# The seam before an output projection: the first tile's order written out, w_out rows staged in output tiles

## The chip, the cores and the metric

The kernel runs on one core of a Trainium2 chip. The metric is the device time of one execution in microseconds. All times below are of this core; the profile is one execution, recorded by the hardware profiler.

## What is computed

One layer of a hybrid backbone, on two inputs: a context of 256 tokens and a latent grid of 2048 tokens, each of width 1024. Both share all weights. Per input:

```python
h = rms_norm(x, g_pre) * (1 + scale) + shift
u = h @ w_in
z, xbc, dt_raw, ga, gb, gsil = jnp.split(u, [I_Z, I_XBC, I_DT, I_GA, I_GB], axis=-1)
y_ssd, h_fin = ssd_branch(z, xbc, dt_raw, ...)        # two scans, forward and backward; rms_norm
y_conf = conformer_branch(ga, gb, ...) * silu(gsil)   # depthwise conv; layer_norm; silu
out = concatenate([y_ssd, y_conf], axis=-1) @ w_out   # 2048 rows of w_out
return x + gate * rms_norm(out, g_post), h_fin
```

The scan runs over chunks of 128 tokens, in both directions. The outputs are the two results and the final scan states of the context. All is float32; each product of the large projections is split into a high and a low half, so that it takes three matmuls (high by high, high by low, low by high).

## The kernel before, in words

The tokens make 18 tiles of 128: tiles 0 and 1 are the context, 2 to 17 the latent grid. For the input projection they are grouped into five blocks (`TOK`, `BNS`, lines 28 and 29): block 0 has 256 tokens, blocks 1 to 4 have 512 each. Block 4 holds tiles 14 to 17, block 3 tiles 10 to 13. Blocks 1, 2 and 0 form the first half, 3 and 4 the second (`ORDER`, line 30). The normalized input of a block (`hh`, `hl`) sits in one of three memory slots, `SLOT` (line 31).

The input projection runs in units, one for each 128 columns of w_in. `silu_unit` (line 560) is the kind that comes last: for each block it runs 24 matmuls of 512 columns into the PSUM tile `sp` and yields after each three, then ScalarE (tanh) and VectorE make the result `sth`, which is stored to DRAM: `ZS` for z, `GS` for the gate. The other work of the time (convolutions, the forward scan) is interleaved with the units' matmuls.

The second pass over the tiles goes backward, `order` = 17, 16, ..., 2, 1, 0 (line 1087). A tile needs, in this pass:

- `ssd_load`, `st_load`: load the scan's pieces `ct`, `el` (twice), `y`, `z` and the chunk state `st`.
- `state_mm` (16 matmuls into `qo`), `y_state`, `y_gate`, `y_sum`: the backward scan's part, gated by z, and the sum of squares `zr`. `state_decay` and `state_add` carry the backward state `Sb` on.
- `conf_load` (`cn`), `conf_sum`, `conf_mean` (matmul `cm`), `conf_centre`, `conf_square`, `conf_sqsum` (`nq`): the layer norm of the other branch.
- `norms` (matmul `pm`, then small VectorE steps and a power on GpSimd), `spread` (matmul `pn`), then `ssd_scale`, `conf_scale`, `conf_silu`, `conf_gate` with the gate `gs_load` loads from `GS`.
- `hl` and `lo`: ScalarE casts the high half, VectorE subtracts for the low half. The result is `yh`, `yl` for the first eight rows of w_out and `ph`, `pl` for the last eight.
- `out_part`: for each of the 16 row groups of w_out, `k`, six matmuls into the PSUM tiles `op`.
- `finish_squares`, `finish_power`, `finish_gate`, `finish_add`: the last norm, the residual and the store.

`load_wo` (line 965) loads row group `k` of w_out into a staging tile `wst` (512 KB) and splits it into `woh` (ScalarE) and `wol` (VectorE). The staging tiles share the tags `yh` and `yl` of pool `p0`. Groups 0 to 8 are loaded during the last units, 9 to 15 after them (lines 1224 and 1225), when the pools of the units are closed and pools `p3` and `wo4` take their memory. Some memory is shared this way at an earlier point also: pool `p2`, which holds the conf tiles, opens when slot 1 is closed, after the first of the two blocks of the last units.

Until line 1243 the compiler orders the instructions of each engine, by priority in program order and a simulated time. From there on (`V.on = S.on = T.on = True`) VectorE, ScalarE and TensorE keep the order of the program, written out in the loop over `order`: the matmuls of tile `i` are cut into pieces, and between them stand the steps of the next tile (`nxt`) and the one after it (`nx2`). The DMAs of the sync queue are not in that list and stay ordered by the compiler. The first tile of the loop, 17, is prepared before it, and so are the scan's and the conf branch's sums of tile 16. The final backward state of the context is written out after the loop by `state_out` (line 1316): eight transposes, two copies on ScalarE, two stores.

Of the kernel before, what the change touches and what calls it, by code (L numbers as in the profile page):

```python
# [17 lines left out]
P = 128  # L18
D = 1024
# [8 lines left out]
TOK = (0, 256, 768, 1280, 1792)  # L28
BNS = (256, 512, 512, 512, 512)
ORDER = ((1, 2, 0), (3, 4))  # L30
SLOT = (0, 1, 2, 1, 2)
RAWO = (2, 260, 772, 130, 642)
NF = 3
PREP = 16
# [27 lines left out]
def take(gen, n):  # L62
    for _ in range(n):
        yield next(gen, None)
# [16 lines left out]
def backbone_kernel(ctx, tc, xa, xt_in, cols, rows, wconv, conf_b, gp_row, bg_row, state0, w_mod, w_dt, w_in, w_out,  # L81
# [796 lines left out]
    def run(gen):  # L878
        for _ in gen:
            pass  # L880
# [36 lines left out]
    xbc_phase(0, first, hb, [hprep(2, hb), hprep(0, hb)], tails, dt_post(0))  # L917
    extra = chain([gate_rows()] + [ctx_conv(j, big) for j in range(4)])
    interleave(post(0, 6), merge(scan(range(9)), 68, extra, 9 + 4 * 13), 90 * 8)
    last = [silu_unit(0, GS0, GS, j, hb, (1, 2, 0)) for j in (6, 7)]  # L920
    prep = hprep(3, hb)
    s = 0
    for b in range(3):
# [38 lines left out]
    p0 = ph_1.enter_context(tc.tile_pool(name="p0", bufs=1))  # L962
    WH, WL = {}, {}

    def load_wo(k, pool):
        wl = pool.tile([P, D], F32R, name=f"wol{k}", tag=f"wol{k}")
        wh = pool.tile([P, D], F32R, name=f"woh{k}", tag=f"woh{k}")
        wr = p0.tile([P, D], F32, tag=("yh", "yl")[k % 2], name=f"wst{k}", bufs=2)
        DMA.dma_start(wr, w_out[k * P:(k + 1) * P, :])
        if k < 8:  # L970
            g = cv[:, C_NORMG + k:C_NORMG + k + 1]
            S.activation(wh, wr, AF.Copy, scale=g)
            V.scalar_tensor_tensor(wl, wr, g, wh.bitcast(F32), MUL, SUB)
        else:
            S.copy(wh, wr)
            V.tensor_tensor(wl, wr, wh.bitcast(F32), SUB)
        WH[k], WL[k] = wh, wl

    y8 = lambda t: t.rearrange("p (q l) -> p q l", l=P)
    Sb = [p0.tile([P, 512], F32, name=f"Sb{g}") for g in range(2)]  # L980
# [42 lines left out]
    def state_add(i):  # L1023
        for g in range(2):
            sg = sl[i]["st"][:, g * 512:(g + 1) * 512]
            if i == NCTX - 1:
                V.tensor_copy(Sb[g], sg)
            else:
                V.tensor_tensor(Sb[g], Sb[g], sg, ADD)
# [21 lines left out]
    def ssd_scale(i, y, pb):  # L1051
        V.tensor_tensor(y, y, rows8(pb[:, 0:P]), MUL)
# [14 lines left out]
    def spread(i, rs):  # L1067
        pb = bank("ss", f"pn{i}")
        for c, r in rs:
            T.matmul(pb[:, c * P:(c + 1) * P], r.to_broadcast([P, P]), ident, start=True, stop=True)  # L1070
        return pb
# [7 lines left out]
    def lo(t):  # L1079
        V.tensor_tensor(t[1], t[2], t[0].bitcast(F32), SUB)  # L1080

    for k in range(6):
        load_wo(k, wo1)
        run(take(blocks, 5))
    state_in(1, Sb, p0.tile([P, 8, P], F32, tag="yl", name="sti1", bufs=2))
    p1 = ph_1.enter_context(tc.tile_pool(name="p1", bufs=1))
# [9 lines left out]
    def conf_load(i):  # L1096
        n = p2.tile([P, 8, P], F32, tag="cn", name=f"cn{i}", bufs=2)
        DMA.dma_start(n, CV[:, i * P:(i + 1) * P].rearrange("(c p) t -> p c t", p=P))
        return n

    def conf_sum(i, n):
        v = p2.tile([P, 8, P], F32, tag="v", name=f"v{i}", bufs=2)
        return v, sum8(v[:, 0, :], v[:, 0:4, :], n)

    def conf_mean(i, t):
        mean = bank("ss", f"cm{i}")[:, 0:P]
        T.matmul(mean, ones, t, start=True, stop=True)
        return mean

    def conf_centre(n, mean):  # L1110
        V.scalar_tensor_tensor(n, rows8(mean), -1.0 / D, n, MUL, ADD)

    def conf_square(v, n):
        S.activation(v, n, AF.Square)
        return v

    def conf_sqsum(i, v):
        return v, sum8(p2.tile([P, P], F32, tag="nq", name=f"nq{i}", bufs=1), v[:, 0:4, :], v)

    def gs_load(i):  # L1120
        gs = p2.tile([P, 8, P], F32, tag="gs", name=f"gsl{i}", bufs=1)
        DMA.dma_start(gs, chan_slice(GS, i))
        return gs

    def conf_scale(n, pb):
        V.tensor_tensor(n, n, rows8(pb[:, P:2 * P]), MUL)
# [6 lines left out]
    def conf_gate(v, gs):  # L1133
        V.scalar_tensor_tensor(v, v, 0.5, gs, MUL, MUL)
# [55 lines left out]
    for g in range(2):  # L1190
        state_decay(i, g)
    state_add(i)
    run(take(blocks, 5))
    for k in range(6, 9):
        load_wo(k, wo2)
        run(take(blocks, 8))
    run(blocks)
    last = [silu_unit(1, GS0, GS, j, hb) for j in range(5, 8)]
    for b in range(2):
        for m, u in enumerate(last):  # L1200
            run(take(u, 8))
            if b == 0 and m == 1:
                rs = norms(i, yz, None)
            if b == 1 and m == 0:
                ssd_scale(i, yz[0], spread(i, rs))
                yh = hl(p0, "y", 2, i, yz[0])
                lo(yh)
                ph_b[1].close()
                p2 = ph_1.enter_context(tc.tile_pool(name="p2", bufs=1))
                n = conf_load(i)  # L1210
                v, t = conf_sum(i, n)
                conf_centre(n, conf_mean(i, t))
    for u in last:
        run(u)
    v, nq = conf_sqsum(i, conf_square(v, n))
    conf_scale(n, spread(i, norms(i, None, (v, nq))))
    gs = gs_load(i)
    conf_silu(n, v)
    conf_gate(v, gs)
    ph_b[2].close()  # L1220
    ph_h.close()
    p3 = ph_1.enter_context(tc.tile_pool(name="p3", bufs=1))
    wo4 = ph_1.enter_context(tc.tile_pool(name="wo4", bufs=1, side="right"))
    for k in range(9, 16):
        load_wo(k, wo4)
    load_gg(0)
    i = order[1]
    ssd_load(i)
    st_load(i)
    n = conf_load(i)  # L1230
    state_mm(i)
    y_state(i)
    y_gate(i)
    yz = y_sum(i)
    for g in range(2):
        state_decay(i, g)
    v2, t = conf_sum(i, n)
    conf_centre(n, conf_mean(i, t))
    nq = conf_sqsum(i, conf_square(v2, n))
    gs = gs_load(i)  # L1240
    ssd_load(order[2])
    n2 = conf_load(order[2])
    V.on = S.on = T.on = True
    for a, i in enumerate(order):
        last = a + 1 == NT
        nxt = order[a + 1] if a + 1 < NT else None
        nx2 = order[a + 2] if a + 2 < NT else None
        banks(i)
        pt = hl(p2, "p", 1, i, v)
        out_part(pso[i], yh, 0, 1)  # L1250
        rs = None if last else norms(nxt, yz, nq)
        if a:
            finish_squares(order[a - 1])
        lo(pt)
        out_part(pso[i], yh, 1, 4)
        if nxt is not None:
            state_add(nxt)
            pb = spread(nxt, rs)
        if nx2 is not None:
            st_load(nx2)  # L1260
            v2, t = conf_sum(nx2, n2)
        if a:
            finish_power(order[a - 1])
        out_part(pso[i], yh, 4, 5)
        if nx2 is not None:
            state_mm(nx2)
        if nxt is not None:
            y = yz[0]
            ssd_scale(nxt, y, pb)
            yhn = hl(p0, "y", 2, nxt, y)  # L1270
            conf_scale(n, pb)
            v = nq[0]
            conf_silu(n, v)
        out_part(pso[i], yh, 5, 8)
        if nx2 is not None:
            mean = conf_mean(nx2, t)
        if nxt is not None:
            lo(yhn)
        if a:
            if order[a - 1] == 1:  # L1280
                load_gg(1)
            finish_gate(order[a - 1])
        out_part(pso[i], pt, 8, 10)
        if nx2 is not None:
            y_state(nx2)
            state_decay(nx2, 0)
            conf_centre(n2, mean)
            conf_square(v2, n2)
        if nxt is not None:
            conf_gate(v, gs)  # L1290
        if nx2 is not None:
            y_gate(nx2)
            state_decay(nx2, 1)
            gs = gs_load(nx2)
            nq = conf_sqsum(nx2, v2)
        if a:
            finish_add(order[a - 1])
        if nx2 is not None:
            yz = y_sum(nx2)
        if a + 3 < NT:  # L1300
            ssd_load(order[a + 3])
            n, n2 = n2, conf_load(order[a + 3])
        else:
            n = n2
        if last:
            out_part(pso[i], pt, 10, 16, (0,))
            out_part(pso[i], pt, 10, 16, (1,))
        else:
            out_part(pso[i], pt, 10, 16)
            yh = yhn  # L1310
    finish_squares(i)
    finish_power(i)
    finish_gate(i)
    finish_add(i, True)
    V.on = S.on = T.on = False
    state_out(1, Sb, lambda n: p1.tile([P, D], F32, tag="z", name=n, bufs=2)[:, 0:512])
    ph_1.close()


# [57 lines left out]
```

## Time and profile before

| | |
|---|---|
| median of 3 runs | 1871.06 us (1869.57 to 1874.34) |
| the profiled execution's own time | 1872.28 us |
| its span, first to last instruction | 1870.5 us |
| mean granted TensorE clock | 0.984 |
| TensorE busy | 1808.1 us (97%) |
| VectorE, ScalarE, GpSimd busy | 1203.1, 863.8, 175.9 us |
| first `op` matmul, last `op` matmul | 1408.3 us, 1862.6 us |

How to read it: PE is TensorE's matmul, PEld its weight load, DVE VectorE, ACT ScalarE, POOL GpSimd, SP the engine that issues most DMAs. Busy times of an engine are sums over its instructions. A row of a timeline has the start, the length, engine and line, the operation, the tile that is written and those that are read, and, in brackets, how long the engine was idle before it and what released it. The chain of work that ended last is followed back from the end: it shows at each time the piece of work on which the end depended, and for DMA the time from issue to landing. Instructions whose order is kept from line 1243 on all carry line 77, that of the helper which records them, so they are told apart by their tiles. Matmuls overlap: one of 512 columns is recorded with 0.39 us, but they start 0.23 us apart.

### The profile page before, as it was taken

The page shows a single profiled execution, that of the slowest core. Times are in us where ns is not written, and L with a number is a line of the kernel's source. Part 1 is how long each engine was busy: PE and PEld are TensorE (multiplying, and loading weights), DVE is VectorE, ACT ScalarE, POOL GpSimd, SP SyncE. Part 2 cuts the span into 40 slices and gives each one's busy share as a digit, 9 for nine tenths or more (in the row PEclk, how much of TensorE's full clock was granted, in tenths as well). Part 3 has the DMA queues.
Part 4 walks back from the last instruction along what each step waited for, and adds up shares of the span by engine and source line. Part 5 has one row for each costly group of instructions (what it writes and reads, how often), then busy time and mean ns, then how long its engine had stood idle before and what let it go on. Part 6 is the DMA issues. An engine that isn't in the chain of part 4 may idle for free.

```text
span 1870.5 us, 30012 instructions
## 1 busy us (share of the span) xinstructions
PE 1808.1 (97%) x11223; PEld 1493.1 (80%) x11223; DVE 1203.1 (64%) x1841; ACT 863.8 (46%) x1956; POOL 175.9 (9%) x281
## 2 busy tenths in 40 slices
PE   7899999999999999999998989999997999999998
PEld 4788887788888888888876767777886888888887
DVE  2477887785555553577587845666347777777773
ACT  3646424455445441644224545553326454444441
POOL 0002001111101100100001111110000111111110
PEclk9899999999999999999999999999998999999999
DMA  8656575576566654545589798895967656666632
GB/s 298 219 199 210 203 241 181 175 254 219 195 217 211 226 196 169 167 155 189 170 200 233 199 251 229 258 244 175 331 189 209 183 167 174 172 171 178 182 106 79
DMA packets 305309, 375.22 MB, mean 201 GB/s; under 512 B 85254, under 2 KB 204678, under 8 KB 305164
## 3 DMA queue, kind: packets, MB, share of 16 engines
q1 hardware_dynamic: 284428, 335.56, 58.1%
q10 hardware_dynamic: 20736, 37.76, 7.1%
q8 instruction: 88, 1.44, 0.3%
q14 instruction: 57, 0.47, 0.1%
HBM read 243.66 MB, written 129.59 MB: 200 GB/s over the span
## 4 chain that ended last, share of the span: by engine, by line
PE 85%; DMA 7%; DVE 4%; ACT 1%; issue 1%; SPq 1%; POOL 0%; POOLq 0%; DVEq 0%; ACTq 0%
PE op L77 21%; PE sp L391 7%; PE sp L392 7%; PE sp L393 7%; PE xp L391 5%; PE xp L392 5%; PE xp L393 5%; PE ga L391 3%; PE ga L393 2%; PE ga L392 2%; PE gb L391 2%; PE gb L393 2%; PE gb L392 2%; DMA lb<-lt 2%; PE py L732 2%; DVE cg L608 2%
## 5 line engine op out<-in xcount | busy, mean ns | idle before, releaser
L696 ACT ACTIVATE lb<-lb,WB 128x128 f32<-128x128 f32 x576 | 184.3, 391 | 167.7 <-POOL lb L688 162.1
L391 PE MATMUL sp<-hh,wh 128*128 128x512 f32 (+1 forms) x640 | 238.5, 373 | 0.0
L392 PE MATMUL sp<-hl,wh 128*128 128x512 f32 (+1 forms) x640 | 236.0, 369 | 0.0
L393 PE MATMUL sp<-hh,wl 128*128 128x512 f32 (+1 forms) x640 | 235.8, 368 | 0.0
L391 PE MATMUL xp<-hh,wh 128*128 128x512 f32 (+1 forms) x480 | 179.3, 375 | 6.1 <-ACT wh L366 4.9
L688 POOL TENSOR_SCALAR_AFFINE_SELECT lb<-lb 128x512 f32<-128x512 f32 x144 | 112.6, 786 | 714.2 <-ACT el L685 366.7
L393 PE MATMUL xp<-hh,wl 128*128 128x512 f32 (+1 forms) x480 | 179.0, 373 | 0.0
L392 PE MATMUL xp<-hl,wh 128*128 128x512 f32 (+1 forms) x480 | 178.9, 373 | 0.0
L488 DVE SCALAR_TENSOR_TENSOR cva<-raw,cwh,cva 128x1280 f32<-128x1280 f32 (+1 forms) x96 | 142.1, 1488 | 19.7 <-ACT cva L482 17.9
L391 PEld LDWEIGHTS sp<-hh,wh 128*128 128x128 f32 x640 | 120.6, 189 | 20.8 <-DVE sth L568 0.4
L393 PEld LDWEIGHTS sp<-hh,wl 128*128 128x128 f32 x640 | 120.6, 188 | 20.7
L392 PEld LDWEIGHTS sp<-hl,wh 128*128 128x128 f32 x640 | 120.7, 189 | 19.8
L391 PE MATMUL ga<-hh,wh 128*128 128x512 f32 (+1 forms) x320 | 122.0, 381 | 6.8 <-DMA wh<-whd 6.3
L391 PE MATMUL gb<-hh,wh 128*128 128x512 f32 (+1 forms) x320 | 121.4, 379 | 5.3 <-DVE gth L555 5.3
L393 PE MATMUL ga<-hh,wl 128*128 128x512 f32 (+1 forms) x320 | 119.4, 373 | 0.5 <-DMA wl<-wld 0.5
L392 PE MATMUL gb<-hl,wh 128*128 128x512 f32 (+1 forms) x320 | 119.6, 374 | 0.0
L393 PE MATMUL gb<-hh,wl 128*128 128x512 f32 (+1 forms) x320 | 119.6, 374 | 0.0
L392 PE MATMUL ga<-hl,wh 128*128 128x512 f32 (+1 forms) x320 | 119.2, 373 | 0.0
L568 DVE SCALAR_TENSOR_TENSOR sth<-sth,sp 128x512 f32<-128x512 f32 (+1 forms) x80 | 50.4, 630 | 97.3 <-ACT sth L567 96.9
L391 PEld LDWEIGHTS xp<-hh,wh 128*128 128x128 f32 x480 | 92.1, 192 | 23.2 <-ACT wh L366 5.5
L608 DVE SCALAR_TENSOR_TENSOR cg<-cg,cv 128x256 f32<-128x256 f32 x240 | 107.6, 487 | 0.6
L392 PEld LDWEIGHTS xp<-hl,wh 128*128 128x128 f32 x480 | 91.7, 191 | 15.7 <-DVE hl L312 0.4
(252 smaller groups left out, 3745.8 us busy)
## 6 DMA issues: line engine op xcount, KB each, us to landing
lb<-lt ACTq DMA_DIRECT2D x144, 256.0 KB, 4.5
wr<-in_w_in SPq DMA_DIRECT2D x88, 256.0 KB, 4.7
whd<-wh SPq DMA_DIRECT2D x44, 512.0 KB, 3.6
wld<-wl SPq DMA_DIRECT2D x44, 512.0 KB, 5.2
wh<-whd SPq DMA_DIRECT2D x44, 512.0 KB, 4.6
wl<-wld SPq DMA_DIRECT2D x44, 512.0 KB, 5.8
xT<-xb SPq DMA_DIRECT2D x18, 512.0 KB, 5.0
yp<-yg SPq DMA_DIRECT2D x36, 256.0 KB, 4.3
```

Of the source, the lines that this page charges most:

```text
L77: return lambda *a, **k: self._tc.keep_in_program_order(f(*a, **k))
L391: T.matmul(ps[:, :BN], wh[:, k, :], hh[:, k, :], start=(k == 0), stop=False)
L392: T.matmul(ps[:, :BN], wh[:, k, :], hl[:, k, :], start=False, stop=False)
L393: T.matmul(ps[:, :BN], wl[:, k, :], hh[:, k, :], start=False, stop=(k == KT - 1))
L488: V.scalar_tensor_tensor(a[:, :n], raw[:, t:t + n], cwh[:, ct * 5 + t:ct * 5 + t + 1], a[:, :n], MUL, ADD)
L568: V.scalar_tensor_tensor(th, th, 1.0, ps[:, :BN], ADD, MUL)
L608: V.scalar_tensor_tensor(acc, g[:, t:t + 256], cv[:, w0 + t:w0 + t + 1], acc, MUL, ADD)
L688: G.affine_select(E[g, hq, d], E[g, hq, d], pattern=[[0, 4], [sg, P]], compare_op=ALU.is_ge, fill=NEG, base=0, channel_multiplier=-sg)
L696: S.activation(lb[:, h, :], lb[:, h, :], AF.Exp, bias=WB[:, i, c + h:c + h + 1])
L732: T.matmul(py[g][j * HD:(j + 1) * HD, q * P:(q + 1) * P], xt[g][:, h * HD:(h + 1) * HD], E[g, hq, 0][:, t, :], start=True, stop=True)
```

## The change

Four things, in one change. Blocks 3 and 4 change places: their slots are swapped, and the last units take block 4 first (in the first half, block 2 first). Tile 16's backward part and both tiles' conf sums are called in between the last units. The loop's first pass, tile 17, is written out ahead of the loop with the kept order already on, and in it stand the splits of row groups 9 to 15, which are loaded into tiles of `p3` (`gg`, `xr` and twice `o`) that the later output steps use. In the second and third tile the steps between the matmuls come later, by `e` = 4 and 2 row groups. And `state_out` is called within the last tile but one.

```diff
-SLOT = (0, 1, 2, 1, 2)
+SLOT = (0, 1, 2, 2, 1)
...
-    last = [silu_unit(0, GS0, GS, j, hb, (1, 2, 0)) for j in (6, 7)]
+    last = [silu_unit(0, GS0, GS, j, hb, (2, 1, 0)) for j in (6, 7)]
...
+    def wo_load(k, pool):
+        WL[k] = pool.tile([P, D], F32R, name=f"wol{k}", tag=f"wol{k}")
+        WH[k] = pool.tile([P, D], F32R, name=f"woh{k}", tag=f"woh{k}")
+        if k < 9:
+            wst[k] = p0.tile([P, D], F32, tag=("yh", "yl")[k % 2], name=f"wst{k}", bufs=2)
+        else:
+            tag = ("gg", "xr", "o", "o")[k % 4]
+            wst[k] = p3.tile([P, D], F32, tag=tag, name=f"wst{k}", bufs=2 if tag == "o" else 1)
+        DMA.dma_start(wst[k], w_out[k * P:(k + 1) * P, :])
...
+    i1 = order[1]
+    ssd_load(i1)
+    st_load(i1)
...
-    last = [silu_unit(1, GS0, GS, j, hb) for j in range(5, 8)]
+    last = [silu_unit(1, GS0, GS, j, hb, (4, 3)) for j in range(5, 8)]
     for b in range(2):
         for m, u in enumerate(last):
             run(take(u, 8))
             if b == 0 and m == 1:
                 rs = norms(i, yz, None)
-            if b == 1 and m == 0:
+                state_mm(i1)
+                y_state(i1)
+                y_gate(i1)
+            if b == 0 and m == 2:
                 ssd_scale(i, yz[0], spread(i, rs))
                 yh = hl(p0, "y", 2, i, yz[0])
                 lo(yh)
+                yz = y_sum(i1)
+                for g in range(2):
+                    state_decay(i1, g)
                 ph_b[1].close()
                 p2 = ph_1.enter_context(tc.tile_pool(name="p2", bufs=1))
-                n = conf_load(i)
-                v, t = conf_sum(i, n)
-                conf_centre(n, conf_mean(i, t))
+                nn = [conf_load(i), conf_load(i1)]
+                vv = [conf_sum(j, n) for j, n in zip((i, i1), nn)]
+                for (v, t), j, n in zip(vv, (i, i1), nn):
+                    conf_centre(n, conf_mean(j, t))
+                    conf_square(v, n)
+                nq = conf_sqsum(i, vv[0][0])
+            if b == 1 and m == 0:
+                rs = norms(i, None, nq)
+                nq = conf_sqsum(i1, vv[1][0])
+            if b == 1 and m == 1:
+                n, v = nn[0], vv[0][0]
+                conf_scale(n, spread(i, rs))
+                conf_silu(n, v)
+                ssd_load(order[2])
+            if b == 1 and m == 2:
+                gs0, v0, n = gs_load(i), v, nn[1]
...
-    for k in range(9, 16):
-        load_wo(k, wo4)
+    for k in range(9, 13):
+        wo_load(k, wo4)
+    n2 = conf_load(order[2])
+
+    def out_seg(i, y, p, k0, k1):
+        out_part(pso[i], y, k0, min(k1, 8))
+        out_part(pso[i], p, max(k0, 8), k1)
...
+    i, nxt, nx2 = order[:3]
+    banks(i)
+    out_part(pso[i], yh, 0, 1)
+    rs = norms(nxt, yz, nq)
+    out_part(pso[i], yh, 1, 4)
+    state_add(nxt)
+    pb = spread(nxt, rs)
+    st_load(nx2)
+    out_part(pso[i], yh, 4, 5)
+    state_mm(nx2)
+    ssd_scale(nxt, yz[0], pb)
+    yhn = hl(p0, "y", 2, nxt, yz[0])
+    conf_gate(v0, gs0)
+    pt = hl(p2, "p", 1, i, v0)
+    gs = gs_load(nxt)
+    conf_scale(n, pb)
+    lo(yhn)
+    lo(pt)
+    out_part(pso[i], yh, 5, 8)
+    for k in (9, 10):
+        wo_split(k)
+        wo_load(k + 4, wo4)
+    v = nq[0]
+    conf_silu(n, v)
+    out_part(pso[i], pt, 8, 9)
+    v2, t = conf_sum(nx2, n2)
+    wo_split(11)
+    wo_load(15, wo4)
+    for k in range(12, 15):
+        wo_split(k)
+    load_gg(0)
+    out_part(pso[i], pt, 9, 12)
+    mean = conf_mean(nx2, t)
+    y_state(nx2)
+    state_decay(nx2, 0)
+    wo_split(15)
+    conf_centre(n2, mean)
+    conf_square(v2, n2)
+    out_part(pso[i], pt, 12, 16)
+    conf_gate(v, gs)
+    y_gate(nx2)
+    state_decay(nx2, 1)
+    gs = gs_load(nx2)
+    nq = conf_sqsum(nx2, v2)
+    yz = y_sum(nx2)
...
-    for a, i in enumerate(order):
+    for a, i in enumerate(order[1:], 1):
         last = a + 1 == NT
+        e = {1: 4, 2: 2}.get(a, 0)
...
-        out_part(pso[i], yh, 0, 1)
+        out_seg(i, yh, pt, 0, 1 + e)
...
-        out_part(pso[i], pt, 8, 10)
+        out_seg(i, yh, pt, 8 + e, 10 + e)
+        if a + 2 == NT:
+            state_out(1, Sb, lambda n: p1.tile([P, D], F32, tag="z", name=n, bufs=2)[:, 0:512])
```

`wo_split(k)` is the second half of the former `load_wo`: the two instructions that make `woh` and `wol` from the staging tile. All other cuts between the pieces of the loop move by `e` in the same way, and `state_out` after the loop is gone.

More of the change, by code (lines that the diff above doesn't have):

```diff
@@ L963, in backbone_kernel, with wo_split @@
     WH, WL = {}, {}
[L965 to L969, printed above, removed]
+    wst = {}
+    def wo_load(k, pool):
[7 more added lines that the diff above has]
+        DMA.dma_start(wst[k], w_out[k * P:(k + 1) * P, :])
+    def wo_split(k):
+        wl, wh, wr = WL[k], WH[k], wst.pop(k)
         if k < 8:
@@ L976, in load_wo @@
             V.tensor_tensor(wl, wr, wh.bitcast(F32), SUB)
-        WH[k], WL[k] = wh, wl
     y8 = lambda t: t.rearrange("p (q l) -> p q l", l=P)
@@ L1082, in backbone_kernel @@
     for k in range(6):
-        load_wo(k, wo1)
+        wo_load(k, wo1)
+        wo_split(k)
         run(take(blocks, 5))
@@ L1192, in backbone_kernel @@
     state_add(i)
+    i1 = order[1]
+    ssd_load(i1)
+    st_load(i1)
     run(take(blocks, 5))
     for k in range(6, 9):
-        load_wo(k, wo2)
+        wo_load(k, wo2)
+        wo_split(k)
         run(take(blocks, 8))
     run(blocks)
-    last = [silu_unit(1, GS0, GS, j, hb) for j in range(5, 8)]
+    last = [silu_unit(1, GS0, GS, j, hb, (4, 3)) for j in range(5, 8)]
     for b in range(2):
@@ L1207, in backbone_kernel @@
                 lo(yh)
+                yz = y_sum(i1)
+                for g in range(2):
+                    state_decay(i1, g)
                 ph_b[1].close()
                 p2 = ph_1.enter_context(tc.tile_pool(name="p2", bufs=1))
-                n = conf_load(i)
-                v, t = conf_sum(i, n)
-                conf_centre(n, conf_mean(i, t))
+                nn = [conf_load(i), conf_load(i1)]
[14 more added lines that the diff above has]
+                gs0, v0, n = gs_load(i), v, nn[1]
     for u in last:
         run(u)
[L1215 to L1219, printed above, removed]
     ph_b[2].close()
@@ L1223, in backbone_kernel @@
     wo4 = ph_1.enter_context(tc.tile_pool(name="wo4", bufs=1, side="right"))
-    for k in range(9, 16):
-        load_wo(k, wo4)
-    load_gg(0)
[L1227 to L1243, printed above, removed]
-    for a, i in enumerate(order):
+    for k in range(9, 13):
[4 more added lines that the diff above has]
+        out_part(pso[i], p, max(k0, 8), k1)
+    V.on = S.on = T.on = True
+    i, nxt, nx2 = order[:3]
[18 more added lines that the diff above has]
+    for k in (9, 10):
+        wo_split(k)
+        wo_load(k + 4, wo4)
[6 more added lines that the diff above has]
+    for k in range(12, 15):
+        wo_split(k)
+    load_gg(0)
+    out_part(pso[i], pt, 9, 12)
[12 more added lines that the diff above has]
+    yz = y_sum(nx2)
+    ssd_load(order[3])
+    n, n2 = n2, conf_load(order[3])
+    yh = yhn
+    for a, i in enumerate(order[1:], 1):
         last = a + 1 == NT
+        e = {1: 4, 2: 2}.get(a, 0)
         nxt = order[a + 1] if a + 1 < NT else None
@@ L1249, in backbone_kernel @@
         pt = hl(p2, "p", 1, i, v)
-        out_part(pso[i], yh, 0, 1)
+        out_seg(i, yh, pt, 0, 1 + e)
         rs = None if last else norms(nxt, yz, nq)
-        if a:
-            finish_squares(order[a - 1])
+        finish_squares(order[a - 1])
         lo(pt)
-        out_part(pso[i], yh, 1, 4)
+        out_seg(i, yh, pt, 1 + e, 4 + e)
         if nxt is not None:
@@ L1261, in backbone_kernel @@
             v2, t = conf_sum(nx2, n2)
-        if a:
-            finish_power(order[a - 1])
-        out_part(pso[i], yh, 4, 5)
+        finish_power(order[a - 1])
+        out_seg(i, yh, pt, 4 + e, 5 + e)
         if nx2 is not None:
@@ L1273, in backbone_kernel @@
             conf_silu(n, v)
-        out_part(pso[i], yh, 5, 8)
+        out_seg(i, yh, pt, 5 + e, 8 + e)
         if nx2 is not None:
@@ L1278, in backbone_kernel @@
             lo(yhn)
[L1279 to L1282, printed above, removed]
-        out_part(pso[i], pt, 8, 10)
+        if order[a - 1] == 1:
+            load_gg(1)
+        finish_gate(order[a - 1])
+        out_seg(i, yh, pt, 8 + e, 10 + e)
+        if a + 2 == NT:
+            state_out(1, Sb, lambda n: p1.tile([P, D], F32, tag="z", name=n, bufs=2)[:, 0:512])
         if nx2 is not None:
@@ L1295, in backbone_kernel @@
             nq = conf_sqsum(nx2, v2)
-        if a:
-            finish_add(order[a - 1])
+        finish_add(order[a - 1])
         if nx2 is not None:
@@ L1308, in backbone_kernel @@
         else:
-            out_part(pso[i], pt, 10, 16)
+            out_seg(i, yh, pt, 10 + e, 16)
             yh = yhn
@@ L1315, in backbone_kernel @@
     V.on = S.on = T.on = False
-    state_out(1, Sb, lambda n: p1.tile([P, D], F32, tag="z", name=n, bufs=2)[:, 0:512])
     ph_1.close()
```

## Prediction

> **What bounds the kernel now.** I read the page's busy shares first, then TensorE busy by stretches of 10 us, then the chain of work that ended last, and last the timeline of the one place where TensorE stands still.
>
> ```profile
> PE 1808.1 (97%) x11223; PEld 1493.1 (80%) x11223; DVE 1203.1 (64%) x1841; ACT 863.8 (46%) x1956; POOL 175.9 (9%) x281
> ```
>
> TensorE is the bound: 97% of a span of 1870.5 us. Other engines matter only where they make it wait. By stretches (columns: length, busy PE, PEld, DVE, ACT, POOL, granted clock, DMA share, GB/s), every stretch from 1200 us to 1860 us holds 9.8 (the first row) to 10.0 us of TensorE work, but for the three that follow it here:
>
> ```profile
> 1340.00:1350.00 10.00, 9.80 (x48) 7.97 (x48) 4.45 (x4) 4.41 (x5) 0.00 (x0) 1.00 1.05 392
> ...
> 1400.00:1410.00 10.00, 9.06 (x51) 7.51 (x49) 6.82 (x11) 5.32 (x14) 0.55 (x1) 1.00 0.72 217
> 1410.00:1420.00 10.00, 0.00 (x0) 0.00 (x0) 6.27 (x7) 9.94 (x20) 0.00 (x0) 0.62 0.92 214
> 1420.00:1430.00 10.00, 7.80 (x30) 6.60 (x31) 7.25 (x14) 2.41 (x3) 2.12 (x2) 0.70 0.88 266
> ```
>
> This is the seam between the last projection units (tile `sp`) and the out-projection (tile `op`). The chain says why it is there, and what a settled tile costs afterwards:
>
> ```profile
> 1404.83 0.24 PE sp L393
> ...
> 1406.44 5.36 DMA gs<-sth
> ...
> 1411.85 4.33 DMA gsl<-gs
> ...
> 1417.42 2.36 DVE wol L976 x2
> ...
> 1422.20 0.98 PE pm L77 x4
> 1423.19 5.64 PE op L77 x18
> ...
> 1449.08 0.34 PE pm L77 x4
> 1449.42 4.25 PE op L77 x18
> 1453.67 0.44 PE pn L77 x4
> 1454.11 1.39 PE op L77 x6
> 1455.50 1.78 PE qo L77 x16
> 1457.29 4.12 PE op L77 x18
> 1461.41 0.22 PE cm L77 x2
> 1461.63 12.29 PE op L77 x54
> ```
>
> The last unit's result goes out to DRAM (5.36) and comes back as the gate of tile 17 (4.33); then VectorE multiplies, splits two w_out rows and sums tile 16's squares; only then can `pm` run, which stands seventh in TensorE's fixed order.
>
> ```profile
> 1406.06 0.49 PE L1070 MATMUL pn<-ident,yr 128*128 128x128 f32 x2 [0.88 <-POOL yr L148]
> ...
> 1406.38 1.95 PE L1014 MATMUL qo<-ct,Sb 128*128 128x128 f32 x16
> ...
> 1408.31 0.70 PE L77 MATMUL op<-woh,yh 128*128 128x512 f32 x2
> ...
> 1409.33 1.28 ACT L1130 ACT_TABLE_LOAD   x1
> ...
> 1410.62 3.18 ACT L1130 ACTIVATE v<-cn,cv 128x128 f32<-128x128 f32 x8
> ...
> 1422.20 0.56 PE L77 MATMUL pm<-ones,zr 128*128 128x1 f32 x2 [12.26 <-DVE zr L986]
> ```
>
> So the seam costs 0.88 + 12.26 us of waits. The restart is slow too: the granted clock is 0.62 and 0.70 there, and from `pm` to `pm` the first tile takes 1449.08 - 1422.20 = 26.88 us, where the eight settled rows sum to 24.83: 2.05 us. Together 15.2 us are to be had, 0.8%. Nothing else on the chain is touched by the change.
>
> **The change part by part.** *The swap of blocks 3 and 4 (slots and order).* Both are 512 tokens wide, so no matmul is added: 0. It stores block 4's gate rows first, so tile 17's gate load no longer follows the last store. That takes 5.36 + 4.33 us out of the chain.
>
> *Tile 16's sums moved into the units.* TensorE's work is the same and only moves: tile 16's `qo` (1.78), `cm` and `pn` (0.22 each), which ran after the last unit, now run before it ends. The last `sp` matmul ended at 1405.07, so the first `op` matmul comes at T0 = 1405.07 + 2.2 = 1407.3. What it waits for has to fit into the second half of the units: 72 matmuls of 12.29/54 = 0.228, or 16.4 us, from 1390.9, when block 4's slot becomes the conf pool.
>
> ```profile
> 1358.64 0.39 SPq L997 DMA_DIRECT2D ct<-xb  x1
> ...
> 1388.24 1.00 SPq L1098 DMA_DIRECT2D cn<-cv  x2
> ...
> DMA to landing us min/median/max: 4.0/5.4/6.1
> ```
>
> Both `cn` loads already go out together at this point, so the sync queue carries nothing new here; tile 16's scan loads (first row) were issued inside the units too. With the latest landing (6.1) they are in at 1397.0. Then VectorE does two sums (1.4 each), two centrings (1.2 each) and two sums of squares (1.4 each): 8.0, ready at 1405.0, with ScalarE's squares beside it. `pm` wants that at T0 + 1.4 = 1408.7: covered, with 3.7 us to spare. If that cover is gone, TensorE waits by the difference.
>
> *The first tile in a fixed order.* This is where new waits can arise: seven w_out rows (9 to 15) are now loaded after T0, and their splits stand in order between tile 17's and 16's steps.
>
> ```profile
> L975 ACT CAST woh<-wst x8: 1027/1050/1054, 1353.9 to 1435.7; 128x1024 fp32r<-128x1024 f32 x8
> L976 DVE TENSOR_TENSOR wol<-wst,woh x8: 1214/1225/1226, 1355.0 to 1436.8; 128x1024 fp32r<-128x1024 f32 x8
> ...
> DMA to landing us min/median/max: 3.6/6.4/8.5
> ```
>
> ```profile
> wst<-in_w_out SPq DMA_DIRECT2D x5, 512.0 KB, 5.0
> ```
>
> The last row is the median landing in 1405 to 1450 us alone, the stretch in question; I use 5.0 and keep 3.6 and 8.5 as ends. From a settled tile come the other durations:
>
> ```profile
> 1483.78 1.28 DVE L77 TENSOR_TENSOR elb<-elb,qo 128x512 f32<-128x512 f32 x2
> 1484.53 2.01 ACT L77 ACTIVATE Sb<-Sb,eTb 128x64 f32<-128x64 f32 x8
> ...
> 1485.09 1.23 DVE L77 TENSOR_TENSOR y<-y,elb 128x1024 f32<-128x1024 f32 x1
> ...
> 1501.61 0.68 DVE L77 TENSOR_TENSOR v<-cn 128x512 f32<-128x512 f32 x1
> ...
> 1502.33 0.75 DVE L77 TENSOR_TENSOR v<-v 128x256 f32<-128x256 f32 x2
> ...
> 1503.83 1.22 DVE L77 TENSOR_TENSOR y<-y,pn 128x1024 f32<-128x1024 f32 x1 [0.48 <-PE pn L77]
> ```
>
> Times after T0. TensorE, by the settled rows, reaches row k=8 at 13.7, k=11 at 17.8, k=13 at 20.8, k=14 at 22.1, k=15 at 23.5 and ends at 24.8; each row's low half (`wol`) is wanted 0.46 later. VectorE waits for `pn` and scales y from 6.8 to 8.0; six steps of 1.2 (gate, conf scale, the low halves of y and p, the splits of rows 9 and 10) bring it to 15.2, the next tile's sum to 16.6. ScalarE casts y and p by 10.2, rows 9 and 10 by 12.2; the silu of tile 16 needs its table again (tanh came between): 1.28 + 3.18, to 16.7; row 11 to 17.7. VectorE ends row 11 at 18.9, TensorE wanted it at 18.3: **0.6 late**. Row 13 reuses row 9's staging tile, free at 14.0: 0.4 to issue, 5.0 to land, cast at 20.4, split at 21.6, wanted at 21.9: in time. Row 14 likewise: 22.8 against 23.2. Then VectorE has `y_state`, 1.28 + 1.23, to 25.3. Row 15 reuses row 11's tile, free at 18.9: landed 24.3, cast 25.3, split 26.5; wanted at 23.5 + 0.46 + 0.6 = 24.6: **1.9 late**. Sum 2.5 us. With a landing of 3.6 row 15 still stands behind `y_state`, so that end stays near 2.5, and below it only if TensorE's own start is late. With 8.5, row 13 is 3.2 and row 15 2.2 late: 6.0. Behind a waiting row load on the sync queue stand the other row loads and tile 16's gate; behind the waiting cast on ScalarE the state decay, due a tile later. POOL has only its short powers.
>
> The table load is the price that speaks against the change, since tanh and silu now alternate: by the row above it took 1.28 us, and the silu started 0.01 us after it. The Trainium skill (ScalarE: Activation LUTs, What ACT_TABLE_LOAD costs) gives 1283 ns for the load and about 2.66 us for a whole switch with its drain. By that, row 11 would be 2.0 us late and the result 1.4 us higher; the trace shows the load alone, and I take the trace.
>
> *Later tiles.* After row 15 VectorE still owes three steps of 1.2 and two sums of 1.4, so tile 15's sums come near T0 + 33. The second tile asks for them only after five rows (before: one), 6.9 us into it, T0 + 34: covered by about 1 us, and a miss costs the difference. The third asks after three.
>
> *The backward state's output* moves from behind the last matmul into the last tile but one.
>
> ```profile
> 1862.84 1.03 PE L162 MATMUL so<-ident,Sb 128*128 128x128 f32 x8
> ```
>
> Eight transposes, 0.9 us start to start, now lie on TensorE's path: +0.9. At the end they hid beside the squares, so nothing comes back; without its two stores the last 7 us gain 0 to 0.5, taken as 0.
>
> **Sum.** Second tile's start before: 1449.08 - 1.4 = 1447.7; after: 1407.3 + 24.8 + 2.5 = 1434.6. That is -13.1, +0.9 makes -12.2. The profiled execution took 1872.28 (span 1870.5 and 1.8 around it), so it would take 1860.1. The median shown is 1.2 us lower, so I forecast 1858.9.
>
> **The rivals.** *Late rows (chance 0.14).* DMA share in the seam is 0.92 and 0.88 already, and the change asks for all seven rows in it. Landings of 8.5 give 6.0 instead of 2.5: 1862.4. Against it: the five rows loaded here before took 5.0.
>
> *Waits inside the units (0.12).* If TensorE's queue takes `cm` right where block 4 ends, it waits for the landing and a sum: 6.1 + 1.4 = 7.5; result 1866.4, hardly different from no change. Against it: the compiled order of before shows no TensorE wait in the units above 0.2 us in a stretch.
>
> *The moved work stays behind the units (0.08),* as `qo` of tile 16 did at 1406.4. Then `pm` waits for qo, three VectorE products, a square and a sum, near 1413, 4.5 us late, and the clock's 2.05 comes back: 1865.5.
>
> *Slower (0.05).* One mechanism: rows 13 to 15, each waiting for its staging tile, find the DMA queue full. Each microsecond of landing above 5.3 is one of TensorE's. From a landing of about 15 us the stall (12.5 by the sums above), the clock's 2.05 and the 0.9 pass what was to be had, 15.2; at 18 us the result is 1874. No w_out landing exceeded 8.5.
>
> **How the numbers follow.** Forecast case 0.61, its own range 1855.5 (no late row, -2.5, and 0.9 hidden) to 1861.5. The first three rivals reach to 1866.4; the range to 1866 leaves out the slower one and part of the second. A change of 0.3%, 5.6 us, is about what can be told apart here: below 1865.5 is faster. Faster 0.61 + 0.14 + about half of the third rival and some of the second: 0.81; same 0.14; slower 0.05.
>
> **What would show it.** Right: stretches 1400 to 1430 at 9 or more of TensorE with the clock at 1.00; `gsl` of tile 17 issued before the last `sp` matmul; two more table loads; the waits left in the seam are for `wol`, at rows 11 and 15; `so` some 40 us before the end; a settled tile still 24.8. Wrong: idle TensorE within the units, a wait ahead of `pm`, landings of `wst` over 8 us, or a second tile that waits for its sums.

## The result, and the profile after

The changed kernel takes 1860.9 us (median of 4 runs, 1857.88 to 1862.99), the kernel before 1872.7 us (4 runs, 1869.57 to 1875.28). The ratio is 0.9938 with a 95% interval of 0.9921 to 0.9954: faster by 0.6%, or 8.6 to 14.8 us. The forecast was 12.2 us less than before; the medians differ by 11.8 us. The profiled execution is the longest of the four: 1862.99 us, span 1861.3.

The stretches of the changed kernel around the seam (columns as before: length, busy PE, PEld, DVE, ACT, POOL, granted clock, DMA share, GB/s):

```profile
1400.00:1410.00 10.00, 9.12 (x47) 7.64 (x46) 7.32 (x12) 3.25 (x5) 0.55 (x1) 1.00 0.49 156
1410.00:1420.00 10.00, 10.00 (x55) 8.57 (x55) 6.71 (x9) 8.25 (x14) 1.59 (x2) 1.00 0.92 317
1420.00:1430.00 10.00, 10.00 (x46) 8.29 (x45) 7.76 (x10) 7.29 (x14) 0.00 (x0) 1.00 0.97 294
1430.00:1440.00 10.00, 8.02 (x26) 5.51 (x25) 9.90 (x12) 5.74 (x15) 0.00 (x0) 0.83 0.68 201
```

The stretch with no TensorE work at all is full now. What is lost has moved to 1430 to 1440, where VectorE is busy 9.9 of 10 us, and the granted clock dips there.

The timeline of the changed kernel has every wait of TensorE that is left between the last unit and the second tile, and the row (`1436.51`) in which the second tile starts:

```profile
1406.40 0.39 PE L393 MATMUL sp<-hh,wl 128*128 128x512 f32 x1
...
1408.01 0.49 PE L1079 MATMUL pn<-ident,yr 128*128 128x128 f32 x2 [0.88 <-POOL yr L148]
...
1409.84 1.28 ACT L1140 ACT_TABLE_LOAD   x1 [2.41 <-DVE cn L1136]
...
1431.17 0.73 PE L77 MATMUL op<-wol,ph 128*128 128x512 f32 x2 [0.31 <-DVE wol L77]
...
1432.92 0.73 PE L77 MATMUL op<-woh,ph 128*128 128x512 f32 x2 [0.56 <-ACT woh L77]
...
1434.77 1.09 PE L77 MATMUL op<-wol,ph 128*128 128x512 f32 x2 [1.11 <-DVE wol L77]
1435.65 1.05 PE L77 MATMUL op<-woh,pl 128*128 128x512 f32 x2
...
1436.51 1.05 PE L77 MATMUL op<-woh,yh 128*128 128x512 f32 x2
```

One wait ahead of tile 17's `pn`, one at w_out row 14, two at row 15; together 2.86 us where the kernel before had 13.14. (Row 8, the first with `ph`, starts at 1421.82, and each row has three pairs of matmuls, so 1431.17 is row 14's second pair.) From 1434.77 on a pair of matmuls is recorded with 1.05 us instead of 0.62: half clock, for 3.4 us. The chain around row 15 (start, length, what) says why the row's low half was late:

```profile
1422.77 6.02 DMA wst<-in_w_out
1428.81 1.06 ACT woh L77
1429.89 1.23 DVE wol L77
1431.12 1.21 DVE elb L77 x2
1432.38 1.11 issue
1433.49 1.23 DVE wol L77
1434.77 9.62 PE op L77 x34
```

Row 14's load, its split, then `y_state` on VectorE (the two `elb` steps, and in the time called "issue" the step that adds them to y), then row 15's subtraction, which TensorE waits for. That is only a part of it, as ScalarE's rows show:

```profile
1429.77 2.02 ACT L77 ACTIVATE Sb<-Sb,eTb 128x64 f32<-128x64 f32 x8
1431.82 1.05 ACT L77 CAST woh<-wst 128x1024 fp32r<-128x1024 f32 x1
```

Row 15's load was issued at 1425.39 and took 6.4 us to land, to 1431.80, when ScalarE had just ended the state decay. The cast ended at 1432.87, and `y_state` held the subtraction back by another 0.6 us, to 1433.49. And the state's transposes stand in the last tile but one:

```profile
1822.95 0.87 PE so L77 x8
```

For the comparisons below I cut the profiled execution at TensorE's marks: the start of the last `sp` matmul, of the second tile, of the fourth tile and of the last `op` matmul. In the kernel before, for instance, the first cut is 1447.56 - 1404.67 = 42.89. These stretches hold only the part that is in question, so they tell apart what the times, which spread by some 5 us from run to run, do not.

| kernel | last `sp` to second tile | second to fourth tile | fourth tile to last `op` | sum |
|---|---|---|---|---|
| before | 42.89 | 49.68 | 365.37 | 457.94 |
| changed | 30.11 | 50.60 | 366.27 | 446.98 |
| row 15 split first | 28.58 | 50.62 | 366.27 | 445.47 |
| rows 13 to 15 not waited for | 26.57 | 51.14 | 366.27 | 443.98 |
| swap undone | 34.38 | 49.69 | 366.27 | 450.34 |
| before, swap alone | 41.74 | 49.92 | 365.37 | 457.03 |
| first tile ordered by the compiler | 38.01 | 49.68 | 366.27 | 453.96 |
| state's output at the end | 29.53 | 49.68 | 365.37 | 444.58 |
| tile 17's `pn` later | 28.10 | 49.68 | 366.27 | 444.05 |
| four edits | 25.98 | 53.36 | 365.37 | 444.71 |
| four edits, sums asked for later | 25.90 | 49.69 | 365.37 | 440.96 |
| before, swap and moved sums alone | 52.68 | 49.68 | 365.37 | 467.73 |
| changed, no shift | 29.50 | 55.02 | 366.27 | 450.79 |

"Before" and "before, swap alone" also run 2.0 us of tile 16's work in the first column, which the others run in the units; so changed against before is 446.98 - (457.94 - 2.0) = -9.0 us in the profiled pair.

### The profile page after: what moved, and what is told of

The parts are those of the page before. It is cut to its first block, busy times and chain, and to the rows that moved or that the text cites. A ratio compares the mean times of both kernels' runs of the same rounds, so it can differ in the third digit from the quotient of the medians.

```text
span 1861.3 us, 30014 instructions
## 1 busy us (share of the span) xinstructions
PE 1810.0 (97%) x11223; PEld 1493.0 (80%) x11223; DVE 1203.1 (65%) x1841; ACT 864.0 (46%) x1956; POOL 170.9 (9%) x281
## 4 chain that ended last, share of the span: by engine, by line
PE 83%; DMA 7%; DVE 5%; issue 2%; ACT 2%; POOL 1%; SPq 0%; POOLq 0%; ACTq 0%; DVEq 0%
PE op L77 20%; PE sp L391 7%; PE sp L392 7%; PE sp L393 7%; PE xp L391 4%; PE xp L392 4%; PE xp L393 4%; PE ga L391 3%; PE gb L391 3%; PE ga L393 3%; PE ga L392 3%; PE gb L393 3%; PE gb L392 3%; DVE cg L608 2%; DMA lb<-lt 2%
## 5 line engine op out<-in xcount | busy, mean ns | idle before, releaser
L688 POOL TENSOR_SCALAR_AFFINE_SELECT lb<-lb 128x512 f32<-128x512 f32 x144 | 107.4, 750 | 717.5 <-ACT el L685 343.2
L700 DVE TENSOR_TENSOR lb<-lb,lb 128x512 f32<-128x512 f32 x72 | 50.3, 699 | 83.3 <-ACT lb L696 64.4
```

Of the source, the lines that this page charges most:

```text
L688: G.affine_select(E[g, hq, d], E[g, hq, d], pattern=[[0, 4], [sg, P]], compare_op=ALU.is_ge, fill=NEG, base=0, channel_multiplier=-sg)
L700: V.tensor_tensor(a, a, E[g, hq, 1], ADD)
```

## The experiments

My theory after the comparison was that what is left in the seam is the lateness of two w_out rows and the half clock behind it (three of the expectations below call them rows 13 and 15; by the timeline they are 14 and 15); that VectorE's sums for the second tile come next; and that of the change's parts the gate's detour is only one of several waits that had stood side by side.

**Row 15's split first.**

```diff
+    wo_split(15)
     y_state(nx2)
     state_decay(nx2, 0)
-    wo_split(15)
```

> The split of w_out row group 15 (cast and subtraction) stands ahead of tile 15's y_state and state decay instead of behind them; nothing else differs from the changed kernel. Theory A: in the changed kernel row 15's split is late because it stands behind 2.0 us of ScalarE and 2.4 us of VectorE work, not because its load lands late. Then TensorE's waits at row 15 (0.56 and 1.11 us) shrink to under 0.7 together, the half-clock window behind them goes (1.7 us), and the first tile is 2 to 3 us shorter: span about 1858.5 against 1861.3. Rival B: the load of row 15, issued at 1425.4, lands only near 1431.8; then the order changes nothing, 0 within 0.5 us, and y_state is late instead.

Measured: ratio to before 0.9931 (0.9916 to 0.9946). The waits in its timeline:

```profile
1431.21 0.73 PE L77 MATMUL op<-woh,ph 128*128 128x512 f32 x2 [0.55 <-ACT woh L77]
1432.47 0.73 PE L77 MATMUL op<-wol,ph 128*128 128x512 f32 x2 [0.53 <-DVE wol L77]
...
1441.20 0.35 PE L77 MATMUL pm<-ones,zr 128*128 128x1 f32 x2 [0.70 <-DVE zr L77]
```

```profile
1430.12 1.05 ACT L77 CAST woh<-wst 128x1024 fp32r<-128x1024 f32 x1 [1.96 <-DMA wst<-in_w_out]
```

Both are row 15's, and row 14 is in time. Row 15's waits fell from 1.67 to 1.08 and the half clock did not come, but 0.70 us came back as a wait of the second tile for tile 15's sum. Net 1.5 us in the stretches, less than theory A's 2 to 3; the intervals of the two times overlap. Both theories hold a part: the order cost something, and the landing, as B had it, the rest, since ScalarE now stood idle until the load was in.

**Rows 13 to 15 not waited for.**

```diff
+    kept = {k: (WH[k], WL[k]) for k in (13, 14, 15)}
+    for k in kept:
+        WH[k], WL[k] = WH[12], WL[12]
     out_part(pso[i], pt, 12, 16)
+    for k in kept:
+        WH[k], WL[k] = kept[k]
```

> The first tile's matmuls of row groups 13, 14 and 15 read row group 12's weights in place of their own (so tile 17's result leaves those three groups out); all loads and splits stay and run as before. This takes the waits for the late rows away without taking any work away. Theory A: what the first tile still loses is these waits (1.98 us of idle TensorE) and one window of half clock that they cause (1.7 us): span 3.7 us lower, about 1857.6, no half-clock stretch at 1434 to 1438. Rival B: the half clock is independent of the waits and comes anyway: 2.0 us lower, about 1859.3. Rival C: VectorE is then the limit and the second tile waits for tile 15's sums: gain under 1 us, a wait ahead of the second tile's pm.

Measured: ratio 0.9923 (0.9905 to 0.9940). Row 14's and 15's waits are gone and the half clock too, 3.5 us less up to the second tile; then the second tile stands before its sum:

```profile
1441.67 0.35 PE L77 MATMUL pm<-ones,zr 128*128 128x1 f32 x2 [1.27 <-DVE zr L77]
```

Together 3.0 us, so A's 3.7 less a part of C. It shows the order of the limits: first the rows, and right behind them VectorE's sums.

**The swap of the blocks undone.** `SLOT` and both orders as before, and the gate's load behind the units:

```diff
-    last = [silu_unit(1, GS0, GS, j, hb, (4, 3)) for j in range(5, 8)]
+    last = [silu_unit(1, GS0, GS, j, hb) for j in range(5, 8)]
...
     for u in last:
         run(u)
+    gs0 = gs_load(i)
```

> The changed kernel with blocks 3 and 4 in their old slots and old order, so that tile 17's gate load must follow the last store of the units; the load is called after the units for that. Theory A: the store and the load (5.4 and 4.3 us) end near 1418.2, the gate is used at 1415.9 in the fixed order, so VectorE and with it ScalarE's cast of ph and the splits of rows 9 to 15 slip by 2.3 us: 2 to 4 us slower than the changed kernel (the slip passes on to rows 13 and 15, with the clock window). Rival B: the whole 9.7 us of the old chain come back: span near 1870.

Measured: ratio 0.9959 (0.9944 to 0.9974); 3.4 us longer than the changed kernel in the stretches. The waits start with the gate's own product and go on at the rows:

```profile
1423.30 0.74 PE L77 MATMUL op<-woh,ph 128*128 128x512 f32 x2 [1.91 <-ACT ph L77]
...
1425.62 0.73 PE L77 MATMUL op<-woh,pl 128*128 128x512 f32 x2 [1.11 <-DVE pl L77]
```

Rows 11, 14 and 15 wait for another 2.6 us in all. Rival B's 9.7 us did not come back. Theory A had the way of it, 2 to 4 us; but that sum held a window of half clock, and here none came, while the changed kernel has one of about 1.5 us. Without it the undone swap costs 4.9 us, more than theory A said.

**The swap alone, on the kernel before.** The same three lines in the other direction.

> The kernel before with the swap of blocks 3 and 4 alone (slots, both orders of the last units). Theory A: the gate of tile 17 is then in memory in time, but ScalarE's silu of that tile ends only at 1413.8, so the multiplication starts 2.4 us sooner than at 1416.3 and the 12.3 us gap shrinks by 2.4 and no more: 1868 to 1869 against 1870.5 span. Rival B: the chain's 9.7 us were the gap; it shrinks by 8 to 10 us: span near 1861, and the rest of the change brings nothing.

Measured: ratio 0.9989 (0.9978 to 1.0000), 10 runs. The gap is nearly all there:

```profile
1414.62 0.56 PE L77 MATMUL pm<-ones,zr 128*128 128x1 f32 x2 [11.04 <-DVE zr L986]
```

11.04 instead of 12.26: it brings 1.2 us of wait, half of theory A's 2.4 and nothing like the chain's 9.7. The gate is in time now, and what ends last is ScalarE, two casts of w_out rows behind the silu and the state decay, and then VectorE:

```profile
1408.78 1.97 ACT L975 CAST woh<-wst 128x1024 fp32r<-128x1024 f32 x2
```

```profile
1409.84 2.36 DVE L976 TENSOR_TENSOR wol<-wst,woh 128x1024 fp32r<-128x1024 f32 x2 [1.14 <-ACT woh L975]
1412.12 0.68 DVE L984 TENSOR_TENSOR v<-v 128x512 f32<-128x512 f32 x1
```

**The swap and the moved sums, with the old first tile.** The kernel before, with the units' part of the change, but rows 9 to 15 staged in the two tags of `p0` by the old `load_wo`:

```diff
     for u in last:
         run(u)
...
+    conf_gate(v0, gs0)
     for k in range(9, 16):
         load_wo(k, wo4)
     load_gg(0)
+    v, gs = v0, gs_load(order[1])
     n2 = conf_load(order[2])
     V.on = S.on = T.on = True
     for a, i in enumerate(order):
```

> The kernel before with the swap of blocks and with tile 16's and 17's sums moved into the units, but with the old first tile: rows 9 to 15 staged in the two tags of p0, their splits placed by the compiler, the loop's first pass as it was, no output tiles for staging. Theory A: the wait for pm goes, but one free staging tile for each tag lets only two rows be under way, and a round trip of load, cast and subtraction takes about 8 us; rows 11, 13 and 15 come late and the seam still costs 6 us or more: span over 1864. Rival B: the moved sums are the whole gain, the old staging keeps up, and the span is that of the changed kernel, 1861.3, or lower since the transposes stay at the end.

Measured: ratio 1.0053 (1.0033 to 1.0074), slower than the kernel before. TensorE stands still for 24 us:

```profile
1435.48 1.40 PE L77 MATMUL pn<-ident,yr 128*128 128x128 f32 x4 [23.96 <-POOL yr L148]
```

```profile
1414.29 5.55 DMA wst<-in_w_out
1419.87 1.05 ACT woh L975
1420.95 1.24 DVE wol L976
1422.20 3.45 DMA wst<-in_w_out
1425.67 1.05 ACT woh L975
1426.74 1.24 DVE wol L976
1428.00 3.43 DMA wst<-in_w_out
1431.45 1.05 ACT woh L975
1432.53 0.98 DVE wol L976
1433.90 1.53 POOL yr L148
```

These lines of its chain are the round trips of the staging tiles, three in a row: load, cast, subtraction, and only then the next load into the same tile. Behind all of them, in the order that the compiler chose, stand the two small VectorE steps that `pn` needs. Theory A's round trips, but the wait is ahead of `pn` and not at the rows, and it has four times the price. So the moved sums are no gain by themselves; in the changed kernel the rows have other staging tiles, and their splits stand behind the steps that TensorE waits for. No run has the old staging with the written order, or the new first tile without the moved sums, so these shares are not told apart any further.

**The first tile ordered by the compiler.**

```diff
-    V.on = S.on = T.on = True
...
     yh = yhn
+    V.on = S.on = T.on = True
     for a, i in enumerate(order[1:], 1):
```

> The changed kernel with the kept order switched on only behind the first tile, so that the compiler orders tile 17's steps by its simulated times; the steps themselves are the same. Theory A: the loss in the first tile comes from when the w_out rows land and from the sum of VectorE's work, not from the written order; the compiler's order gives the same within 2 us of span (1861.3). Rival B: writing the order out is what made the gain; without it TensorE's order is filled with work that is not ready, and the seam costs 5 us or more again: span over 1866.

Measured: ratio 0.9977 (0.9960 to 0.9994). Rival B: the written order is worth 7.0 us in the stretches, with the staging tiles the same.

```profile
1429.43 1.22 PE L1151 MATMUL op<-woh,ph 128*128 128x512 f32 x2 [10.82 <-ACT ph L1085]
```

```profile
1405.94 6.66 DMA gs<-sth
1412.60 0.03 ACTq L985
1412.62 0.04 issue
1412.66 2.95 ACT woh L985 x3
...
1416.93 3.19 ACT v L1140 x8
```

ScalarE had the casts of rows ahead of tile 17's silu, and the first of them waited for the units' last store (6.66 us); tile 17's product came after both.

**The state's output at the end.** `state_out` back behind the loop.

> The changed kernel with the state's output back behind the last matmul. Theory A: the eight transposes (0.87 us on the chain) leave TensorE's path and the stretch from the last matmul to the end stays at 7.5 us, as in the kernel before: 0.9 us faster. Rival B: the two stores and copies at the end delay the last output stores: the tail grows by 0.5 to 1 us and nothing is won.

Measured, one run: 1857.4 us. From the fourth tile to the last `op` matmul 365.37 us instead of 366.27: 0.9 us, theory A. From the start of the last `op` matmul to the end of the span it is 7.5 us, as in both other kernels. By the way it shows a thing about the clock: nearly the same waits as in the changed kernel (0.45, 0.53 and 1.12 us) brought no half clock here, and the stretches up to the fourth tile are 1.5 us shorter.

**Tile 17's `pn` later.**

```diff
-                conf_scale(n, spread(i, rs))
-                conf_silu(n, v)
...
-    n2 = conf_load(order[2])
...
     out_part(pso[i], yh, 0, 1)
+    conf_scale(nn[0], spread(i, rs))
+    conf_silu(nn[0], v0)
+    n2 = conf_load(order[2])
```

> The changed kernel with tile 17's pn, conf scale and silu behind the first six matmuls of the first tile. Theory A: the 0.88 us of idle TensorE ahead of pn goes, and all of tile 17's conf steps come about 0.5 us later on VectorE, which is slack there; the waits at rows 13 and 15 stay at about 2.0 us, since they are set by landings that start after row 9's and 11's splits: 0.5 to 1 us less from the last unit's matmul to the second tile. Rival B: the time won passes into longer waits at rows 13 and 15: 0.

Measured, one run: 1857.29 us. The wait ahead of `pn` is gone, row 15's are the same (0.57 and 1.10). Up to the second tile 28.10 us against 29.53 in the run above, which has no half clock either: 1.4 us, more than the wait alone, since row 14's 0.45 went too.

**No shift in the second and third tile.** `e = 0`.

> The changed kernel with e = 0 in the second and third tile, so that they ask for the next tile's sums after one row as all later tiles do. Theory A: VectorE ends tile 15's sums at 1440.9 in the changed kernel, the second tile's pm would stand at about 1437.5: it waits some 3 us there, and the third tile's less than 1: 3 to 5 us slower than the changed kernel with a window of half clock. Rival B: the shift is not needed, under 1 us.

Measured, one run: 1867.26 us; 3.8 us longer than the changed kernel in the stretches. Theory A, with two windows of half clock where it had one:

```profile
1441.40 0.35 PE L77 MATMUL pm<-ones,zr 128*128 128x1 f32 x2 [2.29 <-DVE zr L77]
```

**Four edits together**: row 15's split first, the low half of tile 16's y behind it, `pn` later, the state's output at the end.

> Four edits on the changed kernel: row 15's split ahead of y_state; the low half of tile 16's y subtracted after that split instead of ahead of row 9's; tile 17's pn, conf scale and silu behind the first row of the first tile (so that TensorE has six matmuls to do while the power runs); the state's output at the end. Theory A: the waits for rows 13 and 15 (2 x 0.5 us left in the run with row 15 alone), the 0.88 us ahead of pn and the 0.9 us of transposes go, and what is left is a wait of the second tile's pm for tile 15's sums, 0.7 us there and up to 2 us here, because VectorE's work up to those sums is unchanged: 3 to 4 us faster than the changed kernel, about 1857.5. Rival B: the rows' landing sets the pace of the first tile: the waits for rows stay and less than 2.5 us are won.

Measured: ratio 0.9941 (0.9925 to 0.9957), no better than the changed kernel. Up to the second tile it is 4.1 us shorter and one wait of 0.18 us is left at the rows, as A had it; then the second tile gives it back:

```profile
1439.92 0.43 PE L77 MATMUL pm<-ones,zr 128*128 128x1 f32 x2 [1.86 <-DVE zr L77]
```

1.86 us and a half-clock window behind them: 53.36 instead of 49.68. The sums that TensorE asks for after five rows come no earlier when TensorE does.

**The same, with the sums asked for one row later.**

```diff
-        e = {1: 4, 2: 2}.get(a, 0)
+        e = {1: 5, 2: 3}.get(a, 0)
...
+    lo(yhn)
     wo_split(15)
-    lo(yhn)
     y_state(nx2)
```

> As the run with four edits, but the second and third tile ask for the sums one row later still (after six and four rows instead of five and three), and the low half of tile 16's y stands just ahead of row 15's split, where VectorE had 1.8 us idle. Theory A: the second tile's pm then waits for nothing or under 0.5 us, so 1 to 1.5 us less than the run with four edits: 4 to 5 us faster than the changed kernel, about 1856.5. Rival B: the wait only moves on (to the third tile's pm or to the next rows): no difference from four edits.

Measured: 1853.64 us (median of 5 runs), ratio to before 0.9909 (0.9893 to 0.9925). In the stretches it is 6.0 us shorter than the changed kernel, and beats both kernels; in the times the interval only just overlaps that of the changed kernel.

```profile
1400.00:1410.00 10.00, 10.00 (x52) 8.44 (x51) 6.85 (x12) 3.09 (x4) 0.55 (x1) 1.00 0.44 138
...
1430.00:1440.00 10.00, 9.89 (x44) 7.87 (x43) 9.28 (x12) 5.84 (x17) 0.00 (x0) 1.00 0.77 214
```

The seam is closed: TensorE works through 1400 to 1430 and is idle for 0.11 us in the stretch after. The heading names one of the run's two edits. The other counts as much, as VectorE's rows show:

```profile
1428.21 1.22 DVE L77 TENSOR_TENSOR yl<-y,yh 128x1024 fp32r<-128x1024 f32 x1
...
1440.14 0.29 DVE L77 TENSOR_TENSOR zr<-z 128x128 f32<-128x128 f32 x1
```

The low half of y now fills a time in which VectorE waited for row 15. Counted from the start of the last `sp` matmul, tile 15's sums end at 33.4 us instead of 34.7 in the run with four edits, and `pm` asks for them at 34.1 instead of 32.9. By these times either edit alone would have left a wait of some 0.7 us; that is an estimate, as no run has only one of them.

## Why the prediction was right, and which terms were off

- *What there was to win.* 15.2 us of waits and slow clock in the seam: right. The last version above has nearly all of it: its sum, 440.96, is 15.0 us under 457.94 - 2.0.
- *Tile 16's sums in the units.* Right: `pm` waited for nothing. The step missed that tile 17's `pn` still waits 0.88 us for its power there, exactly as before; the forecast counted that wait as won. Tile 17's `pm` for the conf branch (1406.86) and its `pn` (1408.01) still run behind the last `sp` matmul.
- *The swap.* I took 9.7 us "out of the chain". As a price of its own that would have been wrong by far: alone it brings 1.2 us of wait, taken out of the changed kernel it costs 3.4 (4.9 if the changed kernel's half clock is left out). The forecast was not hurt, because it summed the whole seam and not the chain's links.
- *The first tile.* 2.5 us of late rows forecast, 1.98 measured, the larger part at row 15 as said (1.9 forecast, 1.67 measured), though `y_state` adds only some 0.6 us of it, since the row also landed late (6.4 us, not 5.0). The other term was wrong: row 11 was not late, because the table was loaded once and not three times. The compiler had put tile 17's silu behind the last tanh (the load at 1409.84 is the only one in the seam), so both silus use it. No run here loads it twice, so the two prices of a switch were not put to the test; the load itself again took 1.28 us. Row 14, for which I had 0.4 us to spare, was 0.31 late: it landed after 6.0 us, and the loads of rows in 1400 to 1440 took a median of 5.6, not 5.0. That the sum of 2.5 comes so near 1.98 is in part luck, with one term too many (row 11, 0.6) and one too few (row 14).
- *The half clock* behind short waits was not in the sum of the forecast case: about 1.5 us in the profiled execution, and none in the run with the state's output at the end, with nearly the same waits.
- *The second tile's sums*, covered "by about 1 us": in the changed kernel the late rows hid it (its `pm` did not wait). Once the rows are in time it is the next limit: 0.70, 1.27 and 1.86 us in three runs.
- *The state's output*: 0.9 us forecast, 0.9 measured, and nothing back at the end.
- *The signs.* TensorE's share (9.12, 10.00 and 10.00 from 1400 to 1430), tile 17's gate load (issued at 1398.0, the last `sp` matmul at 1406.40), a settled tile of 24.8 us and `so` 38 us before the end came as named. The two further table loads and a wait at row 11 did not.

The seam was forecast at -13.1 us. From the last `sp` matmul to the fourth tile it takes 80.71 us in the changed kernel against 92.57 - 2.0 before, or -9.9; in the run with the output at the end, without the half clock, 79.21, or -11.4. Of the 1.7 us between, 0.88 is the wait ahead of `pn`, and some 0.6 are restarts: each of the four waits costs about 0.16 us more than its idle time, since the matmul before it is recorded with 0.39 us and matmuls start 0.23 apart. The late rows are 0.4 less than forecast there (0.45 + 0.53 + 1.12 = 2.10). The rest, some 0.6 us, is not accounted for. The medians (11.8 us less, 12.2 forecast) come nearer to the forecast than the profiled pair does (9.0 less in the stretches); with times that spread by 5 us, that nearness is partly luck. Of the rivals, the slower one, the waits inside the units and the moved work that stays behind them did not come (tile 16's `qo` ran at 1382.2). The rival "late rows" came in small. The run with the swap and the moved sums alone shows that a slower result was near: the same waiting staging tiles as in my slower rival, though there for want of tiles and not for a full DMA queue.

## What to carry to other kernels

When a seam holds several waits side by side, price it by the whole idle time and then ask of each wait what ends next, because taking out the longest link of the chain alone took away 1.2 of 12.3 us here. Work moved ahead of a seam paid here only where what takes its place in the queues behind it (the splits of staged weights) stood behind the steps that the bounding engine asks for, and had other staging tiles; the moved sums came out 0.6% faster with that staging and order and 0.5% slower without them. And each stall that is removed should be followed by a look at the next deadline: four good edits gave nothing until the next sums came 1.2 us sooner and were asked for one row later.

## What the runs showed of the hardware that was not expected

The granted TensorE clock falls to a half for 3.4 us after quite short waits: after 0.31 + 0.56 + 1.11 us in the changed kernel, and after a single one of 1.86 us in the run with four edits. It did not after 0.45 + 0.53 + 1.12 us (the state's output at the end) nor after 1.91 + 1.11 us (the swap undone). The traces say much of why. In each of the 13 the clock changes only at points that lie a whole number of 3.41 us apart, so I count the time without a matmul in each window between two such points. Of the changed kernel:

```profile
1431.54:1434.95 3.41, 1.74 (x7) 0.83 (x6) 3.38 (x5) 1.29 (x3) 0.00 (x0) 1.00 0.31 126
```

Of the run with the state's output at the end:

```profile
1427.60:1431.02 3.42, 1.94 (x7) 0.97 (x6) 3.39 (x5) 2.12 (x6) 0.00 (x0) 1.00 0.41 165
1431.02:1434.43 3.41, 2.79 (x12) 2.33 (x13) 3.41 (x4) 1.06 (x1) 0.00 (x0) 1.00 0.68 152
```

In the changed kernel 1.67 us of one window are idle (3.41 - 1.74), and the clock is at a half from 1434.95 to 1438.36. In the other run a point of this grid, 1431.02, falls into the wait of 1.12 us, so that the windows on its two sides have 1.48 and 0.62 us of idle time, and no half clock follows. Over the 13 traces, from 100 us on, a half clock followed each of the 57 windows at full clock with 2.0 us or more of idle time, and none of the 2987 with less than 1.1 us. Between these bounds it came after some and not after others (after 1.64 us with no shift and 1.86 us with four edits, but not after 1.82 us with the swap undone), and what decides there stays open. So the same waits can cost a window of half clock or nothing, by where they fall on this grid.
